# Tying the side tiles' squares and scalings behind evictions on ScalarE in a hybrid scan kernel

## The chip, the cores and the metric

The kernel runs on one NeuronCore of a Trainium2 chip. The core has five engines with a queue of instructions each: TensorE (in the profile PE for matmuls and PEld for weight loads), VectorE (DVE), ScalarE (ACT), GpSimd (POOL) and SyncE (SP), which issues DMAs. The metric is the device time of one execution in microseconds (us); the median over several runs counts.

## The reference

One layer of a diffusion trunk is computed for 2048 latent tokens with 256 context tokens ahead of them, with a model width of 1024. What matters here is the first part:

```python
def rmsnorm(x, g):
    xf = x.astype(jnp.float32)
    y = xf * lax.rsqrt(jnp.mean(xf * xf, axis=-1, keepdims=True) + EPS)
    return (y * g).astype(x.dtype)
...
hl = modulate(rmsnorm(lat, norm_g[l, 0]), sh1, sc1)
hc = modulate(rmsnorm(cx, norm_g[l, 0]), csh1, csc1)
...
q, zf_fwd, zf_bwd, v, g = jnp.split(h @ w_in, 5, axis=-1)
...
scores = jnp.einsum('bhnik,bhnjk->bhnij', qe, ke)
o_intra = jnp.einsum('bhnij,bhnjv->bhniv', scores, v)
kv = jnp.einsum('bhnjk,bhnjv->bhnkv', k * jnp.exp(b_last - b), v)
```

The tokens are normalised and modulated, and projected to queries, two sets of forget gates, values and output gates for 8 heads. A gated linear recurrence runs over them in both directions, from the state that the context leaves. After it come the output projection, a second normalisation and a gated FFN with a short convolution, which the change does not touch.

## The kernel before

**Stages.** Up to about 62 us of the profile the kernel makes the modulation vectors and the first tokens. The scan's stage goes on to about 1240 us. The output projection, the FFN's two halves and the final normalisation follow.

**The scan.** The 16 tiles of 128 latent tokens are worked on in two groups `g` of 8 tiles; within a group the 8 heads come one after another, and within a head two units of 4 tiles. A projection of a unit (`project`, `step`, L445 to L447) is 8 steps of three matmuls each: tokens and weights are split into a high and a low part. In the first group a head first projects the context (three projections of 256 columns), then gates of unit 0, query 0, gates 1, query 1, value 0, output gate 0, value 1, output gate 1. That is 104 steps for a head.

**What is between the steps.** `tick` counts the steps, and `at(when, f)` puts a small piece of work at a step: the turning of values (`turn`, L607 evicts), the turning of decayed keys (`turned`, L594 evicts `kt`), the scores, the updates of the states (`stepped`: matmul L671 and VectorE's L674), the outputs (matmuls L693 and L696, evicted to `so` in L701). The gates' sigmoid is L494, their scaling L496, the sigmoid of queries and output gates L501, the eviction of values ahead of turning L600. `passed` is a list that holds the gates' scalings, the sigmoids of L501 and the evictions of L600 in the order in which they were written.

**The side tiles.** The first group's tokens stay on the chip. The tokens of tiles 8 to 15, which the second group needs, are prepared on the side, within heads 2 to 5 of the first group, two tiles a head: `make_tok(t)` gives three pieces, at steps 8, 16, 24 for the even tile and 52, 60, 68 for the odd one. The first piece, `load`, takes the tiles `xt` and `hm` (one buffer each), loads 512 KB, and calls `normalize`: a square with a sum on ScalarE (L104, into `hm` as waste), a scaling of the sum on VectorE (L74), a power of -1/2 on GpSimd (L75), and the scaling of the tile on ScalarE (L107). The other two pieces transpose half of it each on TensorE (L116), modulate it (L123 on VectorE for the first half, L120 on ScalarE for the second), split it (L78 and L79) and store it.

**What sets the order.** The kernel is written for a framework with a planner: each engine's queue is filled from instructions that are ready by the planner's model of time, those written earlier first. An instruction written late may thus come far ahead in its engine's queue if its inputs are there by the model. On the chip, each engine works through its queue in that order. `issue_after(x)` adds an order within one queue: what is written in its block comes behind `x` on the engine of `x`.

```python
def put_tok(hm, t, kh):
    b = lp.tile([128, 2, 4, 128], F32R, name="stg", tag="stg", bufs=1)
    split(b[:, 0], b[:, 1], hm[:, 4 * kh:4 * kh + 4])
    sp.dma_start(tok_d[t // UT - 2][kh][:, t % UT], b.bitcast(F32))
...
for n in range(2):
    for i, f in enumerate(make_tok(HT + 2 * (h - 2) + n)):
        at(clock[0] + 8 + 44 * n + 8 * i, f)
```

Of the kernel before, what the change touches and what calls it, by code (L numbers as in the profile page):

```python
# [15 lines left out]
AF = mybir.ActivationFunctionType  # L16
# [5 lines left out]
D = 1024  # L22
# [23 lines left out]
def body(ctx, tc, a, out):  # L46
    nc = tc.nc
    pe, act, dve, pool, sp = nc.tensor, nc.scalar, nc.vector, nc.gpsimd, nc.sync
# [23 lines left out]
    def rms_scale(dst, ss, n, width):  # L72

        dve.tensor_scalar(dst, ss, 1.0 / width, EPS, OP.mult, OP.add)  # L74
        pool.tensor_tensor(dst, dst, mhalf[:, 0:n], OP.pow)  # L75
# [18 lines left out]
    def pool_(stack, name, bufs=1, **kw):  # L94
        return stack.enter_context(tc.tile_pool(name=name, bufs=bufs, reuse_waits="tile", **kw))

    def is_late(h, t):
        return h == NH - 1 and t == NT - 1

    def normalize(xt, junk, stp, on_act=False):  # L100

        ss = stp.tile([128, 1], F32, name="ss", tag="ss", bufs=2)
        rs = stp.tile([128, 1], F32, name="rs", tag="rs", bufs=2)
        act.activation(junk, xt, AF.Square, accum_out=ss)  # L104
        rms_scale(rs, ss, 1, D)
        if on_act:
            act.activation(xt, xt, AF.Copy, scale=rs)  # L107
        else:
            dve.tensor_scalar(xt, xt, rs, None, OP.mult)

    def transpose_mod(xt, hm, g, psp, A, B, tag, bufs, on_act):
# [26 lines left out]
    gp = pool_(c1, "gp", 2)  # L138
# [15 lines left out]
# [6 lines that stand above are left out]
    def x_tile(xt, t):  # L160
        src, r = (a["x"], t) if t >= 0 else (a["ctx"], t + 2)
        sp.dma_start(xt, src[r * 128:(r + 1) * 128])
# [8 lines left out]
    def new_hm():  # L171
        return xp.tile([128, KT, 128], F32, name="hm", tag="hm", bufs=1)

    def load_x(xt, t, hm):
        x_tile(xt, t)
        normalize(xt, hm.rearrange("p k n -> p (k n)"), gp, on_act=True)


    HEAD0 = (2, 1, 3, 0)
# [20 lines left out]
    with ExitStack() as c0:  # L200
# [8 lines left out]
        junk = lp.tile([128, D], F32, name="junk", tag="stg", bufs=1)  # L209
# [37 lines left out]
        for k in range(KT):  # L247
            for c in range(4):
                n = 2 * k + c // 2
# [134 lines left out]
    def mixer_scan():  # L384
# [70 lines left out]
        def project(w, u):  # L455
# [2 lines left out]
            acc(z, w, [cxt[:, kh] if u is None else tok[u, kh] for kh in range(2)])  # L458
            return z

        def make_tok(t):

            got = []

            def load():
                got.append(xp.tile([128, D], F32, name="xt", tag="xt", bufs=1))
                got.append(new_hm())
                load_x(got[0], t, got[1])

            def put(g):  # L470
                transpose_mod(got[0], got[1], g, ps, A1[0], B1[0], "tr", 1, g)
                put_tok(got[1], t, g)

            return load, lambda: put(0), lambda: put(1)
# [12 lines left out]
        passed = []  # L487
# [99 lines left out]
        def turned(kd, s0, n):  # L587

            tr = ps.tile([128, n, 2, 128], F32, name="tr", tag="tr")
            for i in range(n):  # L590
                for d in range(2):
                    pe.transpose(tr[:, i, d], kd[:, d, 4 * (s0 + i):4 * (s0 + i) + 4], ident)
            kt = gp.tile([128, 2, 2, 128], F32, name="kt", tag="kt", bufs=2)
            act.activation(kt[:, 0:n], tr, AF.Copy)  # L594
            return kt

        def values(z, n):

            vt = gp.tile([128, UT, 128], F32, name="vt", tag="vt", bufs=1)
            passed.append(act.activation(vt[:, 0:n], z, AF.Copy).ins)  # L600
            v = gp.tile([128, UT, 128], F32, name="v", tag="v", bufs=2)

            def turn():
                tr = ps.tile([128, n, 128], F32, name="tr", tag="tr")
                for i in range(n):
                    pe.transpose(tr[:, i], vt[:, i], ident)
                act.activation(v[:, 0:n], tr, AF.Copy)  # L607

            return v, turn

# [20 lines left out]
        def unit_steps(h, t0, made):  # L631

            kd, sd, ke, qp, qi, qm, km = made
            kts, states, vs = [], [], []
            at_ = gp.tile([128, UT, 128], F32, name="at", tag="at", bufs=2)
            q_ = act if h == NH - 1 and t0 == NT - UT else sp

            def scores():

                def score(d, s, k, kc, q, qc):  # L640
                    pe.matmul(scs[d][32 * kc:32 * kc + 32, s, 32 * qc.start:32 * qc.stop], k, q,
                              start=True, stop=True, skip_group_check=True)

                kts.append(turned(kd, 0, 2))
                for s in range(UT):
                    for j in range(4):
                        qc = slice(2 - j // 2 * 2, 4 - j // 2 * 2)
                        score(0, s, km[:, s, j], j, qm[:, s, qc], qc)
                    for d in range(2):
                        for j in range(4):  # L650
                            qc = slice(j // 2 * 2, j // 2 * 2 + 2) if j % 2 == 1 - d \
                                else slice(j, j + 1)
                            score(d, s, ke[:, d, 4 * s + j], j,
                                  qp[:, d, 4 * s + qc.start:4 * s + qc.stop], qc)
                kts.append(turned(kd, 2, 2))
                for d in range(2):
                    dve.copy_predicated(ABs[d], masks[d], scs[d])
                made_last.append(dve.tensor_tensor(at_, *ABs, OP.add).ins)

            def stepped(p):  # L660

                if p == 0:
                    states.append(gp.tile([128, UT - 1, 128], F32, name="states", tag="states",
                                          bufs=1))
                kt, v = kts[p], vs[0]
                late = is_late(h, t0 + 2 * p + 1)
                st = [f_state(h, t0)] + [states[0][:, i] for i in range(UT - 1)] + [f_state(h, t0)]
                kv = ps.tile([128, 2, 2, 128], F32, name="kv", tag="kv")
                for d in (1, 0):
                    for i in range(2):  # L670
                        pe.matmul(kv[:, d, i], kt[:, i, d], v[:, 2 * p + i], start=True, stop=True)  # L671
                for i in range(1 if late else 2):
                    s = 2 * p + i
                    dve.scalar_tensor_tensor(st[s + 1], st[s], sd[:, 1, s:s + 1], kv[:, 1, i],  # L674
                                             OP.mult, OP.add)
                sk = gp.tile([128, 2, 128], F32, name="sk", tag="sk", bufs=2)
                act.activation(sk, kv[:, 0], AF.Copy)
                if late:
                    last_kv.append(sk)
                for i in range(1 if late else 2):  # L680
                    s, t = 2 * p + i, t0 + 2 * p + i
                    q_.dma_start(stash[t][:, 0, h], sk[:, i])
                    sp.dma_start(stash[t][:, 1, h],
                                 qi[:, 0, 4 * s:4 * s + 4].rearrange("p g t -> p (g t)"))

            def outputs(p):
                v = vs[0]
                st = [f_state(h, t0)] + [states[0][:, i] for i in range(UT - 1)]
                o = ps.tile([128, 2, 128], F32, name="o", tag="o")
                for i in range(2):  # L690
                    s = 2 * p + i
                    late = is_late(h, t0 + s)
                    pe.matmul(o[:, i], qi[:, 1, 4 * s:4 * s + 4], st[s], start=True, stop=False)  # L693
                    if late:
                        pe.matmul(o[:, i], qi[:, 0, 4 * s:4 * s + 4], Sb[:, h], start=False, stop=False)
                    pe.matmul(o[:, i], at_[:, s], v[:, s], start=False, stop=True)  # L696
                n = 1 if late else 2
                if late:
                    last_out(o[:, 1])
                so = gp.tile([128, 2, 128], F32, name="so", tag="so", bufs=2)  # L700
                act.activation(so[:, 0:n], o[:, 0:n], AF.Copy)  # L701
                for i in range(n):
                    q_.dma_start(stash[t0 + 2 * p + i][:, 2, h], so[:, i])

            def second():
                outputs(0)
                stepped(1)

            return scores, (vs.append, lambda: stepped(0), second, lambda: outputs(1))
# [263 lines left out]
        for g in range(2):  # L973
            for h in range(NH):
# [9 lines left out]
                if g == 1 and h < NH - 2:  # L984
                    n = 7 if h == 0 else 6
# [778 lines left out]
    for i, (j, cs) in enumerate(pieces):  # L1764
# [9 lines left out]
        if cs.start:  # L1774
            v = V[:, j]
# [31 lines left out]
```

## Time and profile before

| | us |
|---|---|
| median of 3 runs | 2758.75 |
| lowest and highest run | 2753.68 and 2759.02 |
| the profiled execution | 2759.34 |
| its span, from the first to the last instruction | 2757.3 |

A row of the timeline gives start, length, engine, line, operation, the tiles written and read, shapes and count; in brackets, if the engine was idle ahead of it, for how long and what ended that. A row of the waits gives who waited and for whom, the sum in us, the number of times and the longest. `L594` is line 594 of the kernel. A row of a stretch gives its bounds, its length, and the busy time of each engine with the number of its instructions.

### The profile page before, as it was taken

What the parts mean: (1) busy time and instruction counts of PE and PEld (TensorE: products, weight loads), DVE (VectorE), ACT (ScalarE), POOL (GpSimd) and SP (SyncE); (2) the same over time, 40 slices, a digit from 0 to 9 for tenths busy, and PEclk for the clock granted to TensorE, in tenths of its full rate; (3) what the DMA queues carried; (4) which work ended last, traced back from release to release, by engine and by line L of the source; (5) the groups of instructions that cost most, each with busy time, mean ns of one, the idle gap of its engine ahead of it and who ended that gap; (6) DMA issues with size and microseconds to landing.
All of it is one profiled execution on the core that took longest, in us unless ns stands there. A gap on an engine that the chain in (4) does not pass through costs nothing. (4 is left out here: it accounts for less than half of the span.)

```text
span 2757.3 us, 42014 instructions
## 1 busy us (share of the span) xinstructions
PE 2708.4 (98%) x16060; PEld 2254.6 (82%) x16060; DVE 1976.0 (72%) x2791; ACT 1129.5 (41%) x1885; POOL 568.2 (21%) x885
## 2 busy tenths in 40 slices
PE   6999999999999999999999999999999999999998
PEld 4888888888888888888887888888888888877887
DVE  4756655566666776668886887777877777586886
ACT  4424443333233233335665444444444444333343
POOL 2111111011111111211220533443434440000001
PEclk9999999999999999999999999999999999999999
DMA  5213323224534443228888222228322234987563
GB/s 230 92 51 100 104 85 100 85 71 168 172 123 136 149 137 112 86 84 295 298 305 323 92 92 68 86 77 305 93 72 81 77 92 151 319 294 249 186 194 122
DMA packets 229104, 410.56 MB, mean 149 GB/s; under 512 B 29604, under 2 KB 137508, under 8 KB 225064
## 3 DMA queue, kind: packets, MB, share of 16 engines
q1 hardware_dynamic: 224584, 398.13, 43.6%
q10 hardware_dynamic: 4320, 9.77, 0.9%
q8 instruction: 126, 2.06, 0.3%
q14 instruction: 74, 0.61, 0.1%
HBM read 293.23 MB, written 114.57 MB: 148 GB/s over the span
## 5 line engine op out<-in xcount | busy, mean ns | idle before, releaser
L445 PE MATMUL z<-tok,w 128*128 128x512 f32 x1280 | 515.4, 403 | 0.0
L447 PE MATMUL z<-tok,w 128*128 128x512 f32 x1280 | 501.0, 391 | 0.0
L446 PE MATMUL z<-tok,w 128*128 128x512 f32 x1280 | 500.8, 391 | 0.0
L79 DVE TENSOR_TENSOR w<-raw,w 128x512 fp32r<-128x512 f32 (+1 forms) x260 | 239.6, 925 | 138.0 <-ACT w L78 134.0
L447 PEld LDWEIGHTS z<-tok,w 128*128 128x128 f32 x1280 | 240.4, 188 | 51.8
L445 PEld LDWEIGHTS z<-tok,w 128*128 128x128 f32 x1280 | 240.7, 188 | 46.0 <-issue 1.7
L446 PEld LDWEIGHTS z<-tok,w 128*128 128x128 f32 x1280 | 241.1, 188 | 45.0 <-DVE tok L79 0.9
L78 ACT ACTIVATE w<-raw 128x512 fp32r<-128x512 f32 (+1 forms) x260 | 196.0, 759 | 138.9 <-PE zd L1061 77.4
L1639 PE MATMUL y<-wd,ml 128*128 128x512 f32 x600 | 234.4, 391 | 2.8 <-DVE ml L79 2.7
L1637 PE MATMUL y<-wd,mh 128*128 128x512 f32 x600 | 233.8, 390 | 2.6 <-ACT X L1672 1.8
L1638 PE MATMUL y<-wd,mh 128*128 128x512 f32 x600 | 233.5, 389 | 0.0
L514 DVE TENSOR_TENSOR_SCAN S<-F,d 128x528 f32<-128x528 f32 (+1 forms) x80 | 91.5, 1143 | 113.3 <-ACT F L496 113.2
L79 DVE TENSOR_TENSOR w<-s,w 128x512 fp32r<-128x512 f32 x126 | 121.3, 968 | 52.8 <-ACT w L78 52.0
L1058 PE MATMUL zc<-rT,w 128*128 128x512 f32 x352 | 137.1, 389 | 1.2 <-DVE uv L1524 1.0
L1060 PE MATMUL zc<-rT,w 128*128 128x512 f32 x352 | 136.9, 389 | 0.0
L1061 PE MATMUL zc<-rT,w 128*128 128x512 f32 x352 | 136.9, 389 | 0.0
L1639 PEld LDWEIGHTS y<-wd,ml 128*128 128x128 f32 x600 | 112.6, 188 | 29.3 <-DVE ml L79 5.9
L1637 PEld LDWEIGHTS y<-wd,mh 128*128 128x128 f32 x600 | 112.6, 188 | 27.0 <-ACT X L1672 2.2
L78 ACT ACTIVATE w<-s 128x512 fp32r<-128x512 f32 x126 | 78.2, 627 | 137.6 <-POOL s L1114 81.0
L75 POOL TENSOR_TENSOR rs<-rs,mhalf 128x1 f32<-128x1 f32 (+3 forms) x53 | 61.7, 1165 | 345.0 <-DVE rs L74 345.0
L1638 PEld LDWEIGHTS y<-wd,mh 128*128 128x128 f32 x600 | 112.6, 188 | 23.2
L1058 PE MATMUL za<-rB,w 128*128 128x512 f32 x336 | 130.7, 389 | 0.0
(353 smaller groups left out, 6246.8 us busy)
## 6 DMA issues: line engine op xcount, KB each, us to landing
raw<-in_w_up_dram SPq DMA_DIRECT2D x88, 512.0 KB, 4.1
raw<-in_w_in_dram SPq DMA_DIRECT2D x80, 512.0 KB, 4.0
lr<-m SPq DMA_DIRECT2D x49, 512.0 KB, 6.0
m<-r SPq DMA_DIRECT2D x66, 256.0 KB, 4.1
spare<-in_w_ada_dram SPq DMA_DIRECT2D x32, 512.0 KB, 4.3
kq<-stash SPq DMA_DIRECT2D x15, 1024.0 KB, 7.8
og<-stash SPq DMA_DIRECT2D x30, 512.0 KB, 5.3
u<-in_w_down_dram SPq DMA_DIRECT2D x51, 256.0 KB, 4.2
```

The lines of the kernel that those rows point to most:

```text
L78: i = act.activation(h, src, AF.Copy)
L79: j = dve.tensor_tensor(l, src, h.bitcast(F32), OP.subtract)
L445: pe.matmul(z, w[:, 0, k], h, start=k == 0, stop=False, skip_group_check=True)
L446: pe.matmul(z, w[:, 0, k], l, start=False, stop=False, skip_group_check=True)
L447: pe.matmul(z, w[:, 1, k], h, start=False, stop=k == KT - 1, skip_group_check=True)
L514: dve.tensor_tensor_scan(flat(S[:, d]), flat(F[:, d]), flat(d1[:, 0:ns]), 0.0, OP.mult, OP.max)
L1058: pe.matmul(o, w[:, 0, k], r[:, :, 0, k], start=start and k == 0, stop=False, skip_group_check=True)
L1060: pe.matmul(o, w[:, 0, k], r[:, :, 1, k], start=False, stop=False, skip_group_check=True)
L1061: pe.matmul(o, w[:, 1, k], r[:, :, 0, k], start=False, stop=k == 3, skip_group_check=True)
L1637: pe.matmul(z, lh, rh, start=start, stop=False, skip_group_check=True)
L1638: pe.matmul(z, lh, rl, start=False, stop=False, skip_group_check=True)
L1639: pe.matmul(z, ll, rh, start=False, stop=stop, skip_group_check=True)
```

## The change

`normalize` gets a pair of instructions, `after`. If it is given, the square comes behind the first of them on ScalarE's queue and the scaling behind the second; ScalarE does both, as before. The side tiles give the pair. For an even tile it is the last eviction of turned values (`v`, L607) and the last eviction of outputs (`so`, L701) written by then; for an odd tile the last eviction of turned keys (`kt`, L594) and the last entry of `passed`. At an even tile's step 8 those two are of the head before; at an odd tile's step 52 they are the `kt` of the context's state in the same head and the sigmoid of the query of unit 0. The other calls of `normalize` give none and are as before.

```diff
-    def normalize(xt, junk, stp, on_act=False):
+    def normalize(xt, junk, stp, after=()):
...
-        act.activation(junk, xt, AF.Square, accum_out=ss)
-        rms_scale(rs, ss, 1, D)
-        if on_act:
-            act.activation(xt, xt, AF.Copy, scale=rs)
+        if after:
+            with tc.issue_after(after[0]):
+                act.activation(junk, xt, AF.Square, accum_out=ss)
+            rms_scale(rs, ss, 1, D)
+            with tc.issue_after(after[1]):
+                act.activation(xt, xt, AF.Copy, scale=rs)
         else:
+            act.activation(junk, xt, AF.Square, accum_out=ss)
+            rms_scale(rs, ss, 1, D)
             dve.tensor_scalar(xt, xt, rs, None, OP.mult)
...
-    def load_x(xt, t, hm):
+    def load_x(xt, t, hm, *after):
         x_tile(xt, t)
-        normalize(xt, hm.rearrange("p k n -> p (k n)"), gp, on_act=True)
+        normalize(xt, hm.rearrange("p k n -> p (k n)"), gp, after)
...
+        evicted = {}
...
-                load_x(got[0], t, got[1])
+                load_x(got[0], t, got[1], *((evicted["kt"], passed[-1]) if t % 2
+                                            else (evicted["v"], evicted["so"])))
...
-            act.activation(kt[:, 0:n], tr, AF.Copy)
+            evicted["kt"] = act.activation(kt[:, 0:n], tr, AF.Copy).ins
...
-                act.activation(v[:, 0:n], tr, AF.Copy)
+                evicted["v"] = act.activation(v[:, 0:n], tr, AF.Copy).ins
...
-                act.activation(so[:, 0:n], o[:, 0:n], AF.Copy)
+                evicted["so"] = act.activation(so[:, 0:n], o[:, 0:n], AF.Copy).ins
```

## The prediction

> **What bounds the kernel now.** I began with the page: it gives the shares of the engines over the span.
>
> ```profile
> span 2757.3 us, 42014 instructions
> PE 2708.4 (98%) x16060; PEld 2254.6 (82%) x16060; DVE 1976.0 (72%) x2791; ACT 1129.5 (41%) x1885; POOL 568.2 (21%) x885
> ```
>
> TensorE works nearly all the time and ScalarE, which the change reorders, 41% of it. So ScalarE's order can matter only where TensorE waits for something behind it. Next, the busy times by stretch; the eight side tiles of the change lie in the first of these two:
>
> ```profile
> 62.00:520.00 458.00, 452.13 (x3549) 386.26 (x3548) 289.98 (x452) 183.21 (x319) 70.53 (x188) 1.00 0.28 88
> 520.00:1250.00 730.00, 729.55 (x5543) 613.82 (x5542) 476.20 (x674) 230.55 (x398) 114.60 (x260) 1.00 0.39 123
> ```
>
> The columns after the length are the busy times of PE, PEld, DVE, ACT and POOL, then clock, DMA share and GB/s. The clock is full. TensorE is idle for 5.9 us in the first stretch and 0.45 us in the second: the same scan without side tiles runs without a gap. Third, the waits of TensorE from 70 to 510 us: all four rows of its matmuls, and the four rows of its weight loads for the same instructions.
>
> ```profile
> PE kv L671 <- ACT v L607: 3.3, 3, 1.1
> PE o L693 <- DVE states L674: 0.8, 1, 0.8
> PE kv L617 <- ACT kt L594: 0.7, 2, 0.5
> PE kv L671 <- ACT sk L677: 0.4, 1, 0.4
> ```
> ```profile
> PEld kv L671 <- ACT v L607: 4.6, 3, 1.5
> PEld kv L617 <- ACT kt L594: 2.3, 5, 0.9
> PEld o L693 <- DVE states L674: 1.0, 1, 1.0
> PEld kv L671 <- ACT sk L677: 0.9, 2, 0.5
> ```
>
> The matmul waits are seven and sum to 5.2 us. Idle time counts from the modelled end of the matmul before, and these are pipelined:
>
> ```profile
> 264.99 0.39 PE L446 MATMUL z<-tok,w 128*128 128x512 f32 x1
> 265.22 0.39 PE L447 MATMUL z<-tok,w 128*128 128x512 f32 x1
> 266.72 1.16 PE L671 MATMUL kv<-v,kt 128*128 128x128 f32 x8 [1.11 <-ACT v L607]
> 267.95 0.40 PE L446 MATMUL z<-tok,w 128*128 128x512 f32 x1
> ```
>
> A matmul lasts 0.39 us but the next starts after 0.23, so each wait delays the stream by its idle time plus 0.16: here 266.72 - 265.22 - 0.23 = 1.27 us. All seven: 5.2 + 7 x 0.16 = 6.3 us. That is the most that mending these waits can give if everything later moves up with it.
>
> **The change part by part.** It adds and removes no work: the 8 squares (L104), 8 scalings (L107), the loads and all else stay. It only forbids ScalarE's queue to hold a square or a scaling ahead of four kinds of eviction. The ties are orders within one queue, so I take them at no instruction; bounds are 0 and, if each of 16 ties made an event instruction as the scalings have one now, 16 x 0.017 = 0.3 us on ScalarE.
>
> ```profile
> L107 ACTq EVENT_SEMAPHORE  x8: 17/17/17, 85.6 to 468.2; - x8
> ```
>
> *Even tiles 10, 12, 14 (three places alike).* ScalarE now, with VectorE's step in between:
>
> ```profile
> 258.56 1.06 ACT L104 ACTIVATE hm<-xt 128x1024 f32<-128x1024 f32 x1 [0.67 <-DVE stg L79]
> 265.03 1.15 ACT L107 ACTIVATE xt<-xt,rs 128x1024 f32<-128x1024 f32 x1 [2.65 <-POOL rs L75]
> 266.09 0.58 ACT L607 ACTIVATE v<-tr 128x512 f32<-128x512 f32 x1
> 263.80 0.14 DVE L74 TENSOR_SCALAR rs<-ss 128x1 f32<-128x1 f32 x1
> ```
>
> The scaling stands ahead of the eviction of the turned values. It waits 2.65 us for its factor, because L74 on VectorE came 4 us after the square, behind that engine's own work. TensorE needs `v` and stands 1.27 us. With the change the scaling is behind the `so` that was traced last, a head later; `v` runs as soon as its transposes are done, over 2.65 us earlier. The wait needed 1.27, so all of it goes: 3 x 1.27 = 3.8 us. What is late next there is VectorE's part of the next scores, and heads without side tiles show no wait on it.
>
> *Odd tiles 9, 11, 13, 15.*
>
> ```profile
> 467.05 1.06 ACT L104 ACTIVATE hm<-xt 128x1024 f32<-128x1024 f32 x1 [1.14 <-DMA xt<-in_x_dram]
> 468.10 0.58 ACT L594 ACTIVATE kt<-tr 128x512 f32<-128x512 f32 x1
> 468.73 0.94 PE L617 MATMUL kv<-v,kt 128*128 128x128 f32 x6 [0.47 <-ACT kt L594]
> ```
>
> Here the square is ahead of the turned keys: it waits for its DMA, runs 1.06 us, and the context state on TensorE waits for `kt`. Tied behind `kt`, it gives the two places of the row above: 0.7 + 2 x 0.16 = 1.0 us. The scaling goes behind the query's sigmoid.
>
> *Tile 8, hoisted as far as head 0.*
>
> ```profile
> 81.74 1.06 ACT L104 ACTIVATE hm<-xt 128x1024 f32<-128x1024 f32 x1
> 91.85 1.15 ACT L107 ACTIVATE xt<-xt,rs 128x1024 f32<-128x1024 f32 x1 [5.67 <-POOL rs L75]
> 92.91 0.58 ACT L494 ACTIVATE F<-z 128x512 f32<-128x512 f32 x1
> 90.62 0.39 PE L447 MATMUL z<-tok,w 128*128 128x512 f32 x1
> 95.61 1.25 DVE L514 TENSOR_TENSOR_SCAN S<-F,d 128x528 f32<-128x528 f32 x1
> 104.01 0.33 DVE L674 SCALAR_TENSOR_TENSOR states<-Sf,sd,kv 128x128 f32<-128x128 f32 x1
> ```
>
> ScalarE stands 5.67 us before the scaling. The gate's last matmul starts at 90.62 and is done at 91.01; its sigmoid starts at 92.91. Without the scaling it starts 1.9 us earlier, VectorE's scan after it too, and VectorE's queue down to the states up to as much. TensorE waits there 0.8 and 0.4 us, so both can go: 1.2 + 2 x 0.16 = 1.5 us. Bounds: 0, if VectorE's later work holds the states, and 1.5; I take 1.5, since 1.9 exceeds either wait.
>
> *Where the work goes.* Square behind `v`, scaling behind `so`, at tile 10's new place (first six rows), and the scaling of an odd tile (last two):
>
> ```profile
> 282.31 0.60 ACT L607 ACTIVATE v<-tr 128x512 f32<-128x512 f32 x1 [0.19 <-PE tr L606]
> 286.23 0.38 ACT L677 ACTIVATE sk<-kv 128x256 f32<-128x256 f32 x1 [3.32 <-DVE states L674]
> 291.88 0.39 ACT L701 ACTIVATE so<-o 128x256 f32<-128x256 f32 x1 [0.53 <-PE o L696]
> 292.92 0.38 ACT L494 ACTIVATE F<-z 128x256 f32<-128x256 f32 x1 [0.65 <-PE z L447]
> 295.60 0.60 PE L116 MATMUL tp<-ident,xt 128*128 128x128 f32 x4
> 298.28 0.45 POOL L528 COPY TB<-S 128x4 f32<-128x4 f32 x1 [33.28 <-DVE S L514]
> 236.68 0.60 ACT L501 ACTIVATE q<-z 128x512 f32<-128x512 f32 x1 [3.99 <-PE z L447]
> 242.12 0.60 ACT L494 ACTIVATE F<-z 128x512 f32<-128x512 f32 x1 [4.84 <-PE z L447]
> ```
>
> The square fits the 3.32 us idle ahead of `sk` (282.9 to 284.0). GpSimd is idle for 33 us there, so the factor can be ready by 286. The scaling runs from 292.27 to 293.42. Queued behind it are the context's gate sigmoid, up to 0.5 us later, and through it VectorE's scan, not TensorE. The tile's transposes need it at 295.60: 2.2 us to spare. So 0, with bounds of 0 and 4 x 0.5 = 2 us if the sigmoid's delay reached TensorE. The odd scaling fits 4.84 us idle: 0. Loads stay where they are on SP's queue: a tile's buffer is free when the tile before is transposed, which no tie moves. On VectorE's and GpSimd's queues L74 (0.14 us) and L75 move along with each square, to places where GpSimd waits for nothing else.
>
> *Sum.* 3.8 + 1.0 + 1.5 = 6.3 us off. The profiled execution took 2759.34 us (2.0 around its span): 2753.0. The median of the three runs is 2758.75, 0.6 lower, and gives 2752.5. That is 0.23% faster; 0.2%, 5.5 us, is about what a measurement of this kernel can tell from no change.
>
> The same sum by weight loads is 4.6 + 2.3 + 1.0 + 0.9 = 8.8 us, and 2750.5. I take matmul starts instead: the loads' rows hold five `kt` waits, three of which held up no matmul. The Trainium skill's "Perfetto Trace Analysis", section "Identifying the Most-Contended Engine", says that matmul busy time misleads, since pipelined matmuls "look smaller in the trace", and would have headroom judged by weight loads; by that, the 8.8 would be the sum. No run here has shown that yet.
>
> **The rivals.**
>
> *Only the even places give (3.8 us, 2755.5).* For it: from the scan at 95.61 to the states at 104.01 lie 8.4 us of VectorE's queue, any of which may hold the states, and the 1.0 of `kt` rests on half a microsecond per place. Against: ScalarE's 5.67 us is a plain cause.
>
> *The larger sum (8.8 us, 2750.5)*, as worked out above.
>
> *Nothing comes of it (2759.3).* TensorE arrives early and waits later for what does not move up. For it: DMA is the only thing not driven by TensorE. Against: DMA share is 0.28 and 0.39, and TensorE has 0.45 us idle from 520 to 1250.
>
> *Slower: the factor comes late at the new place.* If L75 stood on GpSimd's queue behind the copy that begins at 298.28 and lasts 0.45, the scaling of 1.15 could end at 299.9 at the earliest, and the transposes would stand 4.3 us. After 5.64 us of waiting TensorE also runs slowly:
>
> ```profile
> 1496.56 0.80 PE L1058 MATMUL zd<-rT,w 128*128 128x512 f32 x1 [5.64 <-ACT w L78]
> 1497.16 0.63 PE L1060 MATMUL zd<-rT,w 128*128 128x512 f32 x1
> ```
>
> 0.63 us against 0.40 after the wait of 1.11 above. Leaving that aside, the four even tiles give 4 x 4.3 - 6.3 = 10.9 us more, 2770.2. It decides from 1.6 us a tile on, where the gain is gone, and makes it slower by 0.2% from 3.0 us on. Against: the square ends 14 us before those copies, and nothing else is queued on GpSimd. The Trainium skill's "TensorE: Matmul & The Clock Gate", section "Why this matters for your kernels", puts the limit for idle gaps at about 3 us; the two rows agree. By it this rival would cost more still.
>
> **How the numbers follow.** Full sum 0.58; even places alone 0.20; larger 0.05; nothing 0.07; slower 0.10. The full sum passes the 0.2% by little, so 0.46 of its 0.58 counts as faster, with 0.05 of the larger and 0.04 of the partial: 0.55. Same: 0.12 + 0.16 + 0.07 = 0.35. Slower: 0.10. Predicted is 2753.0. The range goes from 2748 (the larger sum, less half of the 5.3 us between the runs at 2753.68 and 2759.02) to 2759.5 (nothing gained).
>
> **What would show it.** Right: no TensorE wait on `v`, `kt` or the states between 70 and 510 us; squares of even tiles right behind L607 and scalings right behind L701; no square in head 0; from 62 us to the same point TensorE's idle below 1 us. Wrong: a new wait of the transposes L116 on L107, of L120 or L123 behind it, or of TensorE on the gates' evictions; VectorE still late for the states in head 0; or a different order of the loads on SP.

## The result and the profile after

| | before | after |
|---|---|---|
| median of 6 runs, us | 2758.81 | 2747.55 |
| lowest and highest, us | 2753.68 and 2759.02 | 2746.22 and 2752.72 |
| the profiled execution, us | 2759.34 | 2752.72 |
| its span, us | 2757.3 | 2750.7 |

The ratio is 0.997, with a 95% interval of 0.996 to 0.998: faster by 0.3%. The means of the six runs give 0.997 too, the two medians 0.996. Ratios here and below leave out the one slow run, of 3389.09 us with only the even tiles tied. The profiled execution of the changed kernel is the slowest of its six, so the two profiles are 6.6 us apart and the two medians 11.3. The experiments below say what of this is the change.

The busy times by stretch of the changed kernel, in the columns of the prediction, and the waits of TensorE's matmuls from 70 to 510 us:

```profile
62.00:520.00 458.00, 457.35 (x3588) 392.50 (x3587) 291.20 (x452) 185.62 (x323) 66.26 (x188) 1.00 0.28 89
520.00:1250.00 730.00, 727.45 (x5525) 610.83 (x5524) 480.06 (x682) 230.67 (x401) 116.37 (x261) 1.00 0.40 127
```
```profile
core 0 of [0], span 2750.7 us
engine line waited for: us in total, times, longest us
```

The list of waits is empty: all seven are gone, and TensorE's idle time in the scan's first half is 0.65 us where it was 5.9. In the second stretch it is 2.55 us where it was 0.45, because the stage behind the scan now begins within it: up to 1240 us it is 0.46. VectorE, ScalarE and GpSimd do the same work as before (2791, 1885 and 885 instructions in both traces). ScalarE's timeline at tile 10, first the place that the tile has left, then the one it has come to (L106, L109, L614 and L708 are the L104, L107, L607 and L701 of before):

```profile
259.21 0.60 ACT L607 ACTIVATE vt<-z 128x512 f32<-128x512 f32 x1 [3.89 <-PE z L451]
261.01 0.60 ACT L614 ACTIVATE v<-tr 128x512 f32<-128x512 f32 x1 [1.20 <-PE tr L613]
...
278.38 0.60 ACT L614 ACTIVATE v<-tr 128x512 f32<-128x512 f32 x1 [0.19 <-PE tr L613]
278.88 1.05 ACT L106 ACTIVATE hm<-xt 128x1024 f32<-128x1024 f32 x1
...
287.96 0.38 ACT L708 ACTIVATE so<-o 128x256 f32<-128x256 f32 x1 [0.53 <-PE o L703]
288.24 1.15 ACT L109 ACTIVATE xt<-xt,rs 128x1024 f32<-128x1024 f32 x1
289.28 0.37 ACT L501 ACTIVATE F<-z 128x256 f32<-128x256 f32 x1
```
```profile
280.29 0.54 POOL L75 TENSOR_TENSOR rs<-rs,mhalf 128x1 f32<-128x1 f32 x1 [29.20 <-DVE rs L74]
```
```profile
262.65 0.40 PE L451 MATMUL z<-tok,w 128*128 128x512 f32 x1
262.89 0.83 PE L678 MATMUL kv<-v,kt 128*128 128x128 f32 x6
291.67 0.60 PE L120 MATMUL tp<-ident,xt 128*128 128x128 f32 x4
```

The turned values are evicted 1.20 us after the eviction ahead of them, waiting only for their own transposes, and `kv` follows the last projection after 0.24 us instead of 1.50. The factor is done on GpSimd at 280.8, 7.4 us ahead of the scaling, which does not wait. The scaling ends at 289.4, and the transposes come at 291.67.

In head 0 the gate's sigmoid, now L501, starts at 88.80 and VectorE's states at 101.41:

```profile
84.69 0.60 ACT L614 ACTIVATE v<-tr 128x512 f32<-128x512 f32 x1 [1.20 <-PE tr L613]
88.80 0.60 ACT L501 ACTIVATE F<-z 128x512 f32<-128x512 f32 x1 [3.51 <-PE z L451]
```
```profile
101.41 0.33 DVE L681 SCALAR_TENSOR_TENSOR states<-Sf,sd,kv 128x128 f32<-128x128 f32 x1
```

Before, they started at 92.91 and 104.01. This trace runs 0.9 us ahead already at 62 us, so the sigmoid has gained 3.2 us and the states 1.7.

### The profile page after: what moved, and what is told of

Read it like the earlier page. It is cut to its first block, busy times and chain, and to the rows that moved or that the text cites. A ratio compares the mean times of both kernels' runs of the same rounds, so it can differ in the third digit from the quotient of the medians.

```text
span 2750.7 us, 42006 instructions
## 1 busy us (share of the span) xinstructions
PE 2705.6 (98%) x16060; PEld 2253.6 (82%) x16060; DVE 1974.7 (72%) x2791; ACT 1128.9 (41%) x1885; POOL 563.3 (20%) x885
```

## The experiments

A measure that single executions don't blur was needed. Two fixed matmuls were found by their place in TensorE's order, those that start last before 62 and before 520 us in the kernel before, and the time between their starts was read in each trace. It is called the scan's stretch here. The bounds at 2440 and 2600 us are two more matmuls, found in the same way; the rest goes to the end of the span. All the traces of this study:

| trace | until 62 us | scan's stretch | from there to 2440 us | 2440 to 2600 us | rest |
|---|---|---|---|---|---|
| before, first trace | 61.80 | 458.13 | 1919.94 | 160.06 | 157.38 |
| before, second trace | 62.15 | 457.99 | 1921.32 | 154.04 | 155.94 |
| only tile 8 tied | 61.81 | 455.86 | 1919.35 | 159.88 | 155.94 |
| only tiles 10, 12, 14 tied | 60.85 | 454.19 | 1920.07 | 159.36 | 156.52 |
| only odd tiles tied | 61.19 | 456.71 | 1919.20 | 156.56 | 155.94 |
| changed, first trace | 60.93 | 451.09 | 1920.22 | 161.34 | 157.09 |
| changed, second trace | 61.86 | 451.01 | 1920.12 | 158.30 | 155.94 |
| changed, third trace | 61.17 | 451.04 | 1918.44 | 157.74 | 156.05 |
| only the squares tied | 61.00 | 451.01 | 1918.60 | 159.29 | 155.92 |
| only the scalings tied | 60.96 | 451.83 | 1920.85 | 160.41 | 156.14 |
| scaled on VectorE, no tie | 61.62 | 451.86 | 1918.38 | 158.79 | 155.94 |
| changed, transposes early | 61.99 | 452.12 | 1918.42 | 160.77 | 155.93 |

The theory of the prediction, A: each wait of TensorE that goes is worth its own length, and nothing else moves. Rival B: VectorE's own queue holds the states in head 0. Rival C, formed on seeing 11.3 us between the medians: the new order shortens later stages too.

**One part alone.** The pair of ties is given for some of the tiles only; `tie` is `issue_after`, or nothing for `None`.

```diff
-                load_x(got[0], t, got[1], *((evicted["kt"], passed[-1]) if t % 2
-                                            else (evicted["v"], evicted["so"])))
+                pair = (evicted["kt"], passed[-1]) if t % 2 else (evicted["v"], evicted["so"])
+                load_x(got[0], t, got[1], *(pair if t == 8 else (None, None)))
...
+                load_x(got[0], t, got[1], *(pair if t in (10, 12, 14) else (None, None)))
...
+                load_x(got[0], t, got[1], *(pair if t % 2 else (None, None)))
```

> Only tile 8 is tied (square behind the turned values, scaling behind the outputs); tiles 9 to 15 are as before. Theory A (each wait that goes is worth its own length, nothing else moves): the two TensorE waits at 104 and 105 us (on the states, 0.8, and on sk, 0.4) go, the five others stay; the scan's stage is 1.5 us shorter, the time about 0.05% lower, which the timed runs alone can't tell from none. Theory B (VectorE's own queue holds the states): the two waits stay, 0 us. Theory C (the scan's new order also shortens later stages): the time falls by 5 us or more although only 1.5 us go in the scan.

> Only tiles 10, 12 and 14 are tied. Theory A: the three TensorE waits on the turned values go, the waits on kt (0.7 in two) and the two of head 0 stay; the scan's stage is 3.8 us shorter, the time 0.14% lower. Theory B says the same of this part. Theory C: the time falls by 8 us or more.

> Only tiles 9, 11, 13 and 15 are tied. Theory A: the two TensorE waits on kt go, the three on v and the two of head 0 stay; the scan's stage is 1.0 us shorter, the time 0.04% lower. If the weight loads' waits were the measure, it would be up to 2.3 us. Theory C: the time falls by 5 us or more.

The times: 2754.25, 2752.88 and 2753.10 us against 2754.74 of the kernel before on that chip, with ratios of 0.9998 (0.999 to 1.0007), 0.9989 (0.998 to 0.9998) and 0.9993 (0.9984 to 1.0001). Only the even tiles can be told from no change by the times, and only just. TensorE's waits from 70 to 510 us tell more; tile 8 alone, the even tiles alone, the odd tiles alone (the lines of these kernels are ten further down than those of before: L617 is its L607):

```profile
PE kv L681 <- ACT v L617: 3.3, 3, 1.1
PE kv L627 <- ACT kt L604: 0.3, 1, 0.3
```
```profile
PE o L703 <- DVE states L684: 0.8, 1, 0.8
PE kv L627 <- ACT kt L604: 0.7, 2, 0.4
PE kv L681 <- ACT sk L687: 0.4, 1, 0.4
```
```profile
PE kv L681 <- ACT v L617: 3.3, 3, 1.1
PE o L703 <- DVE states L684: 0.8, 1, 0.8
PE kv L681 <- ACT sk L687: 0.4, 1, 0.4
```

Each part takes away its own waits and leaves the others. Against the mean of the two traces of before, 458.06, the even tiles give 3.9 us in the scan's stretch and the odd ones 1.4. Tile 8 gives 2.2, of which 1.6 lie at 100 to 110 us, where its two waits were. The other 0.6 are at tiles it does not touch, where the waits on `kt` differ from execution to execution: 0.3 in one place in this trace, 0.7 in two in the first. 1.6 + 3.9 + 1.4 = 6.9 of the 7.0 us that the whole change takes off. Followed matmul by matmul against the first trace of before, the changed kernel gains 1.6 us at tile 8's place, 1.4 at each of the three waits on `v` (4.1 in all) and 1.3 at the four places of the odd tiles, which makes up its 7.0. In the trace of the even tiles alone, the three places gain the same 4.1, and 0.2 go again at a wait on `kt` that those tiles do not touch. Theory B has fallen: the states came early enough once the scaling was gone.

**The changed kernel again.**

> The changed kernel once more. Theory A: from 62 to 520 us of the kernel before, the scan is 6.3 to 6.8 us shorter as in the first trace; whatever else the time differs by lies before 62 us or after 1240 us, at other places in this trace than in the first one, and the time is 6 to 7 us lower apart from that. Theory C: the scan's stage is the same as in the first trace, and the later stages are again shorter, by the same amount at the same places, 11 us in all.

> The changed kernel a third time, for the size of the effect and a third trace. Theory A: 62 to 520 us of the kernel before take 451.0 us again (7.1 us less), to 0.2 us, and the time is 7 to 9 us lower; the stretches before 62 us and behind 1240 us differ from both other traces.

2746.73 us against 2754.74, ratio 0.9968 (0.9956 to 0.998), and 2746.39 against 2754.45, ratio 0.9973 (0.9964 to 0.9982). The scan's stretch is 451.01 to 451.09 in all three traces, whatever the execution's time; that is 7.0 us off, more than the 6.3 to 6.8 expected of the second. Outside it the same kernel differs by several us: the stretch from 2440 to 2600 us took 161.34, 158.30 and 157.74.

**The kernel before again.**

> The kernel before once more, for a second trace. Theory A (what differs outside the scan's stage is the spread of single executions): from 62 to 520 us it takes the 458.1 us of the first trace, to 0.3 us; the stretch behind 2440 us takes another time than the 317.4 us of the first trace, as it did in the traces of p_tile8, p_odd and the changed kernel, whose order there is the same; the ratio is 1 within 0.1%. Theory C (the change shortens later stages): the stretch behind 2440 us takes 317 us again.

2756.03 us against 2754.78, ratio 1.0002 (0.9993 to 1.0011). The scan's stretch is the same to 0.15 us, and 2440 to 2600 us took 154.04 us after 160.06. TensorE's waits from 2440 us on: the first trace of the changed kernel, and the second of the kernel before.

```profile
PE y L1646 <- DVE ml L79: 4.0, 4, 2.5
PE y L1644 <- DVE P L1698: 0.7, 1, 0.7
```
```profile
core 0 of [0], span 2751.4 us
engine line waited for: us in total, times, longest us
```

One execution of the kernel before has no such wait at all. So theory C finds no support: behind the scan the changed kernel is now longer, now shorter than the kernel before, by no more than either differs from itself. The 2758.81 us of the first comparison is the highest median of the kernel before in four sessions; the others are 2754.74, 2754.78 and 2754.45 (28, 32 and 15 runs).

**One tie of the two.** The square's alone, `(pair[0], None)`, and the scaling's alone, `(None, pair[1])`, for all eight tiles.

> All eight tiles, but only the square's tie; the scaling goes where the planner puts it, which is right behind the square in the even tiles. Theory D (what matters is that neither instruction stands ahead of v or kt): the factor is ready 1 us after the square and ScalarE is idle there for 3 us, so no wait of TensorE comes back and the scan is 7 us shorter as in the changed kernel. Theory E (the scaling's tie behind the outputs is needed too, since the scaling would hold up sk or the gates): waits of TensorE on sk, kt or F, and a gain of 5 us or less.

> All eight tiles, but only the scaling's tie; the squares stay where they are in the kernel before. Theory D: the waits of TensorE on v (3.3) and those of head 0 (0.8 and 0.4) go, since the scaling was what held the queue there; the waits on kt stay, since the square held it there: 3.9 + 1.6 = 5.5 us of the scan. If the squares of the even tiles cost anything where they are, it is less.

The squares' tie alone: 2747.49 against 2754.78, ratio 0.9972 (0.9963 to 0.9981); scan's stretch 451.01, no wait of TensorE. Its ScalarE at tile 10, where L109 is the square and L112 the scaling:

```profile
278.91 1.05 ACT L109 ACTIVATE hm<-xt 128x1024 f32<-128x1024 f32 x1
279.86 0.19 ACT L109 ACTIVATION_READ_ACCUMULATOR hm<-xt 128x1 f32 x1
280.90 1.15 ACT L112 ACTIVATE xt<-xt,rs 128x1024 f32<-128x1024 f32 x1 [0.84 <-POOL rs L75]
282.26 0.39 ACT L687 ACTIVATE sk<-kv 128x256 f32<-128x256 f32 x1 [0.21 <-DVE states L684]
```

The planner now puts the scaling right behind the square, where it waits 0.84 us for its factor in time that ScalarE has to spare. Theory D holds, and the scaling's tie is not needed beside the square's. The scalings' tie alone: 2749.25, ratio 0.9976 (0.9967 to 0.9985); scan's stretch 451.83, 6.2 us off where D had 5.5. The `v` waits and those of head 0 are gone. One wait on `kt` is left:

```profile
PE kv L627 <- ACT kt L604: 0.2, 1, 0.2
```

It is smaller than expected, though the squares stand ahead of `kt` as before. The difference is at tile 15's place, and the traces show what it hangs on. There the square waited 1.14 us for the load of its tile in the first trace of before; here the load is in time, and the square waits only until the tile before has been split and its buffer is free:

```profile
459.91 1.06 ACT L109 ACTIVATE hm<-xt 128x1024 f32<-128x1024 f32 x1 [0.77 <-DVE stg L79]
```

From issue to landing this load took 4.9 us in the first trace of before and with the even tiles alone, 4.5 in the second trace of before, and 4.1 to 4.2 here, with tile 8 alone and with the scaling on VectorE. Against the first trace of before, the place took 0.05 us less with the even tiles alone, 0.4 less in the second trace of before, and 0.7 less in the other three. So what the square costs `kt` hangs on when the load of its tile lands.

**The scaling on VectorE.** No ties; `gp, on_act=False` instead of `True` in `load_x` of the kernel before.

> The kernel before without ties, but the side tiles are scaled on VectorE (0.75 us each) and not on ScalarE. Theory D: ScalarE waits for no factor any more, so the waits on v and those of head 0 go, and the waits on kt (squares) stay; VectorE takes 6 us more and now waits for the factor itself in the middle of its busiest stretch, so part of the gain may come back as waits of TensorE on the scores or the states: 2 to 5.5 us off in the scan. If instead the mere work on ScalarE had been the cause and not its wait, the waits on v would stay at about half.

2748.27 against 2754.78, ratio 0.9975 (0.9967 to 0.9983); scan's stretch 451.86, 6.2 us off, more than expected. One wait on `kt` of 0.2 us is left here too. VectorE at tile 10:

```profile
262.22 0.69 DVE L580 TENSOR_TENSOR qp<-qp,rt 128x512 f32<-128x512 f32 x1
263.35 0.75 DVE L109 TENSOR_SCALAR xt<-xt,rs 128x1024 f32<-128x1024 f32 x1 [0.43 <-POOL rs L75]
264.88 0.35 DVE L674 SCALAR_TENSOR_TENSOR states<-Sf,sd,kv 128x128 f32<-128x128 f32 x1 [0.78 <-PE kv L671]
```

VectorE waits 0.43 us for the factor behind its last piece for the scores and then 0.78 us for TensorE: the scaling fits a gap that was there. The squares stayed on ScalarE, and the waits on `v` went all the same, so the scaling cost them and not the square. This run takes the scaling's wait for its factor and its work off ScalarE together and does not part them; the rows do. In the trace of before the scaling could have run from 262.38 to 263.53 if its factor had been there. The eviction of the turned values starts 1.80 us after the eviction ahead of it in the changed kernel (259.21 and 261.01), which would be 263.58 in the trace of before (261.78 for the one ahead). So the work would just have fitted, and it is the wait of 2.65 us at the head of ScalarE's queue that cost the time. That is an estimate from these rows; no run tried it.

**How much room the scaling has.** The changed kernel with the even tiles' first transposes at step 1 after the load, not 8:

```diff
-                            at(clock[0] + 8 + 44 * n + 8 * i, f)
+                            at(clock[0] + 8 + 44 * n + (8 * i if n or i != 1 else 1), f)
```

> The changed kernel, but the first transposes of each even tile come at step 1 after its load and not at step 8, which is about 2.4 us earlier on TensorE's queue. It tests the 2.2 us to spare at the scaling's new place. If that is right, TensorE now waits for the scaling at four places, 0.2 to 0.6 us each, and the scan is 1 to 2.5 us longer than the changed kernel's 451.0 us. If there is more to spare, no wait appears; if the scaling comes later than I read it, the waits are 1 us or more each.

2750.93 us in one run, which tells nothing; scan's stretch 452.12, 1.1 us longer than the changed kernel's. ScalarE's scaling and TensorE's transposes at tile 10, and the waits of the weight loads:

```profile
289.59 1.14 ACT L109 ACTIVATE xt<-xt,rs 128x1024 f32<-128x1024 f32 x1
```
```profile
290.50 0.28 PE L449 MATMUL z<-cxt,w 128*128 128x256 f32 x1
290.79 0.66 PE L120 MATMUL tp<-ident,xt 128*128 128x128 f32 x4
```
```profile
PEld tp L120 <- ACT xt L109: 0.8, 4, 0.2
```

The scaling ends at 290.73 and the transposes start at 290.79, 0.29 us after the matmul ahead of them instead of some 0.12. Four places wait 0.2 us each. So the room was about 2.2 us, as read, and TensorE begins to wait from there on. That is how the slower rival would have begun.

## Why the prediction was right, and where it was not

- *The sum by the starts of matmuls, 6.3 us:* right in kind, 0.7 to 0.8 short. The scan's stretch lost 7.0 to 7.1 us in three traces.
- *Even tiles, 3.8:* measured 3.9, and 4.1 at the three places themselves. *Tile 8, 1.5:* measured 1.6; the bound that the prediction set against it, VectorE's queue, does not act. The sigmoid there moved by 3.2 us, not 1.9: the matmul at 90.62 that was quoted as the gate's last belonged to the projection behind it. *Odd tiles, 1.0:* measured 1.4. This is the term that was furthest off. Five weight loads had waited for `kt`, of which the term counted the two with a wait of a matmul; and the planner, knowing `kt` to be earlier, now puts the context's `kv` three matmuls earlier in TensorE's order at all four places, which I had not seen coming. Against the first trace of before, the odd tiles alone gain 1.2 us at the two places that the term counted and no more than 0.1 at each of the other two. How much of this the new order of the matmuls makes is not shown.
- *The sum by weight loads, 8.8:* too large by 1.7 to 1.8. Of these waits 1.3 us are still there in the changed kernel (1.0 on `kt`, 0.3 on `sk`), at no cost that the matmuls show; the 7.5 that went are 0.4 to 0.5 more than what was gained, and the starts of matmuls 0.7 to 0.8 less. Idle time between matmuls, 5.2 us, was too small a measure. The Trainium skill's "Perfetto Trace Analysis", section "Identifying the Most-Contended Engine", prefers weight loads to matmul busy time as a measure of TensorE's headroom, and says nothing of single waits; here the weight loads were the nearer of the two only once what stays was taken off.
- *New places at no cost:* right. The scaling held up the context's gate sigmoid by about 0.3 us there and no wait of TensorE came of it.
- *The time, 2753.0 us, with 2748.0 at the low end:* the median came out at 2747.55, just below the range. The step that failed is the base of the sum. The profiled execution of before, 2759.34 us, lay 4 to 5 us above the medians of the later sessions, and the range allowed for that only half of the difference between two runs, below the larger sum. What made the first session's executions longer is not shown. The ratio forecast was 0.9977; measured were 0.997, 0.9968 and 0.9973, each with an interval of 0.1% to either side. 7.1 us of 2754.5 would be 0.9974, and 2754.5 less 7.0 is 2747.5, the median of the result.
- *What would show it:* the `v`, `kt` and states waits gone, idle below 1 us, squares behind the turned values, scalings behind the outputs, no square in head 0, loads at their places. All of it came.
- *The rivals:* "only the even places" fell with the tile 8 and odd runs, "nothing comes of it" with the time, and "slower" with the factor at 280.3, 14 us ahead of the copies on GpSimd that the rival had put in its way.

## What to carry to other kernels

An instruction put early into an engine's queue because its first input is there can hold up everything behind it when its second input comes late, so look for a wait whose releaser is an engine with plenty of idle time, and ask what stands ahead of the releasing instruction. Size a wait of TensorE by the starts of the matmuls on either side and compare it with the waits of the weight loads, less those that will stay: here the first came out low at all three terms and the second a little high, while idle time gave 5.2 us of 7.0. Where single executions differ by more than the change is worth, compare the time between two fixed instructions in several traces.

## What had not been expected of the hardware

The scan's stretch repeats to 0.15 us between executions of one kernel, while 160 us of the last stage, the same instructions in every kernel here, differ by up to 7.3 us (154.04 to 161.34). In the executions with waits there TensorE waits mostly for VectorE's split of left factors, and in some for VectorE's sums or ScalarE's evictions; from 2435 to 2600 us, two traces of either kernel move 230 to 243 GB/s by DMA, the one without waits the most. What is late where TensorE waits, and whether it is a transfer, stays open.
